# A decoder layer on one core: where q is normalized, when q and k are transposed, and two smaller moves in the order of work

## The chip, the cores and the metric

The kernel runs on one core of a Trainium2 chip. The core has five engines with a queue each: TensorE (PE, matrix products; its weight loads are shown apart as PEld), VectorE (DVE), ScalarE (ACT), GpSimd (POOL) and SyncE (SP, which here issues all DMAs). Each works through its own instructions in order and waits on semaphores for the others. The metric is the device time of one execution in microseconds (us), lower is better.

## The reference, cut to what matters

One layer on x of 256 tokens by 1024 features, float32. Two mixers work side by side, a feed-forward network follows:

```python
h = rmsnorm(x, norm_mix_g)
q, k, v, u_pool, gate_logits = split(h @ w_in)          # 512, 512, 512, 512, 2048 columns
q = rotary(rmsnorm(heads(q), q_norm_g))                 # 8 heads of 64; norm over the 64
k = rotary(rmsnorm(heads(k), k_norm_g))
attn = softmax(causal(q @ k.T * 64**-0.5)) @ v          # 256 tokens are one block, so plain causal attention
pooled = multiscale_pool(u_pool)                        # trailing means over 2, 4, 8, 16 tokens
gates = sigmoid(gate_logits + b_gate)
x = x + (gates[0] * (attn @ w_branch_attn) + gates[1] * (pooled @ w_branch_pool)) @ w_out
h2 = rmsnorm(x, norm_ffn_g)
gate, val = split(causal_conv3(h2 @ w_up))              # 2 x 2816 columns
return x + (silu(gate) * val) @ w_down
```

The norm of q multiplies each head of each token by one number. The rotation is linear and acts within a head, so this number may be applied before it, after it, or to the row of logits.

## The kernel before, in words

**Products.** Activations lie feature by token (128 features on the partitions, 256 tokens along the row), and nearly every weight product is done in three single-pass products: both operands are split into a high part (type fp32r, written by ACT, `high`, line 82) and a low part (the rest, written by DVE, `low`, lines 86 and 88), and `mm3` (lines 94 to 96) adds high by high, high by low and low by high. A product of 128x128 weights by 256 tokens is one PE instruction. Scores, transposes, value products and a few small products are plain float32.

**Weights.** They come in chunks of 1 MB (128x2048). A chunk is split in two pieces of 1024 columns. `next_high` puts a piece's high part on ACT, `next_low` its low part on DVE (one piece behind, STAGGER), and with the last piece of a chunk it issues the DMA of the chunk four places on (`load`). `ahead(n)` does one such pair, and a second one if fewer than n pieces are ready in front of the chunk in use. These calls stand in the program where the author put them, and every engine runs its instructions in exactly this order (the loop at line 714 ties each engine's instructions to program order).

**Stages in order.** q, k and v are projected with tokens on the partitions (`project`). While k and v run, `norm_evacuate` (line 287) takes q and k out of PSUM: ACT squares, DVE multiplies with the token's norm and the gain and sums the squares for each head, POOL raises the mean square to the power -0.5 (line 300), multiplies the 512 columns with it (line 301) and rotates 16 columns of each head (lines 306 to 311). Then come four tiles of pool features (`ps_u`), 16 tiles of gates (`ps_g`, n = 0 to 15), eight tiles of the pool branch (`ps_bp`), eight of the attention branch (`ps_ba`), eight of the output projection (`ps_out`), and the feed-forward stage (`ps_up`, `ps_d`).

**Attention between them.** `to_heads` (line 314) transposes q or k for one half of the tokens: four 128x128 transposes on PE into a bank, one copy on ACT. q's two calls stand after the second `ps_u` tile, k's two after the first gate tile. Before gate tiles 2, 6, 10 and 14 `scores` handles two heads: scores on PE, then on DVE mask, row maximum and the factor -1/8 (lines 438 to 443), on ACT four exponentials with their sums (line 447), on DVE a reciprocal, on POOL the product with it (line 453). Four tiles later `weigh` transposes the result on PE (line 461), and some tiles after that `values` multiplies with v (line 472), and ACT and DVE write `ath` and `atl`. The last `values` comes after the sixth `ps_bp` tile.

**Branches.** Each `ps_ba` tile goes through DVE (line 558, product with the gate), POOL (line 559, sum), ACT (`mh`) and DVE (`ml`), and the output projection reads `mh` and `ml` of all eight tiles: the first two of its tiles run over seven of them before the eighth. `settle` (line 522) is a float32 product ahead of the seventh `ps_bp` tile; its result is read by nobody.

**Residuals.** `residual(j)` (line 577) adds `ps_out` to x on DVE, writes the high part `hhi` and a square on ACT, adds the square to `ss2` on POOL, calls `ahead`, and writes `hlo` on DVE. The first feed-forward tiles run over seven of the eight features, then the token norm R2 is prepared (`ps_n`: line 242, line 245 on POOL, line 249 on DVE, line 253 on PE), then they take the eighth.

PSUM has eight banks of 2 KB a partition: the pool `mm` has four (`bank`), `ps2` two tiles of two banks.

Of the kernel before, what the change touches and what calls it, by code (L numbers as in the profile page):

```python
# [8 lines left out]
F32 = mybir.dt.float32  # L9
F32R = mybir.dt.float32r  # L10
AF = mybir.ActivationFunctionType
ALU = mybir.AluOpType
AX = mybir.AxisListType

P = 128
S = 256
NT = S // P
D = 1024
KD = D // P
H = 8  # L20
DH = 64
AW = H * DH
KA = AW // P
# [7 lines left out]
EPS = 1e-6  # L31
# [20 lines left out]
AHEAD = 4  # L52
FFN_AHEAD = 6
KREADY = 0
FIRST = 2
HOME = 24
LEAD = 104
XCUTS = (1, 2, 3, 4, 6, 8)

# [2 lines left out]
def hybrid_layer_kernel(ctx: ExitStack, tc: tile.TileContext, xq_d, par_d, wkv_d, wpg_d,  # L62
                        wpool_d, wba_d, wbp_d, wout_d, wup_d, wdn_d, out_d):
    nc = tc.nc

    const = ctx.enter_context(tc.tile_pool(name="const", bufs=1))
# [8 lines left out]
    tmp = mixer.enter_context(tc.tile_pool(name="tmp", bufs=2))  # L75

    def bank(name):
        return mm.tile([P, 512], F32, tag="mm", name=name)
# [84 lines left out]
    def ahead(upto=0):  # L163

        next_high()
        next_low()
        if at[1] - sum(p[0] < used[0] for p in pieces) < upto:
            next_high()
            next_low()
# [104 lines left out]
    def project(name, hook, pt=None):  # L274
# [9 lines left out]
            hook(k)  # L284
        return pt

    def norm_evacuate(pt, t, gcol, name):
        r = rtok1[:, t:t + 1]
        g = par[:, None, gcol:gcol + DH].to_broadcast([P, H, DH])
        p3 = pt.rearrange("p (h d) -> p h d", d=DH)  # L290
        qg = tmp.tile([P, 2, 3 * P], F32, tag="big", bufs=4, name=f"qg_{name}{t}")
        qg = qg.rearrange("p a b -> p (a b)")[:, 0:AW].rearrange("p (h d) -> p h d", d=DH)
        q2 = tmp.tile([P, H, DH], F32, tag="q2", bufs=1, name=f"q2_{name}{t}")
        nc.scalar.activation(q2, p3, AF.Square, scale=r)
        nc.vector.scalar_tensor_tensor(qg, p3, r, g, ALU.mult, ALU.mult)
        ss = tmp.tile([P, H], F32, tag="ss", name=f"ss_{name}{t}")
        nc.vector.tensor_reduce(ss, q2, axis=AX.X, op=ALU.add)
        nc.vector.tensor_scalar(ss, ss, 1.0 / DH, EPS, op0=ALU.mult, op1=ALU.add)
        rh = tmp.tile([P, H], F32, tag="rh", name=f"rh_{name}{t}")
        nc.gpsimd.tensor_tensor(rh, ss, mhalf[:, 0:H], ALU.pow)  # L300
        nc.gpsimd.tensor_tensor(qg, qg, rh[:, :, None].to_broadcast([P, H, DH]), ALU.mult)
        cos = par[:, None, C_COS + t * ROPE:C_COS + (t + 1) * ROPE].to_broadcast([P, H, ROPE])
        sin = par[:, None, C_SIN + t * ROPE:C_SIN + (t + 1) * ROPE]
        ta = tmp.tile([P, H, ROPE], F32, tag="ropea", name=f"ra_{name}{t}")
        tb = tmp.tile([P, H, ROPE], F32, tag="ropeb", name=f"rb_{name}{t}")
        nc.gpsimd.tensor_tensor(ta, qg[:, :, 0:ROPE], cos, ALU.mult)
        nc.gpsimd.tensor_tensor(tb[:, :, 0:HALF], qg[:, :, HALF:ROPE],
                                sin[:, :, 0:HALF].to_broadcast([P, H, HALF]), ALU.mult)
        nc.gpsimd.tensor_tensor(tb[:, :, HALF:ROPE], qg[:, :, 0:HALF],
                                sin[:, :, HALF:ROPE].to_broadcast([P, H, HALF]), ALU.mult)  # L310
        nc.gpsimd.tensor_tensor(qg[:, :, 0:ROPE], ta, tb, ALU.add)
        return qg

    def to_heads(qg, t, dst, name):
        pq = bank(f"ps_t{name}{t}")
        flat = qg.rearrange("p h d -> p (h d)")
        for j in range(KA):
            nc.tensor.transpose(pq[:, j * P:(j + 1) * P], flat[:, j * P:(j + 1) * P], ident)
        nc.scalar.activation(dst[:, :, t * P:(t + 1) * P], pq.rearrange("p (j c) -> p j c", c=P), AF.Copy)

    def on_q(k):
        if k % 2 == 1:
# [19 lines left out]
    def on_v(k):  # L342
        if k % 2 == 1:
            ahead()
        if k == 1:
            kg.append(norm_evacuate(ptk[0], 0, C_KG, "k"))
        if k == 3:
            kg.append(norm_evacuate(ptk[1], 1, C_KG, "k"))

    qg, kg, stat = [], [], []  # L350
    ptq = project("q", on_q)
# [56 lines left out]
    for b in range(2):  # L408
        w = chunk("p")
        for c in range(2):  # L410
            ps = feature_tile(w, c, f"u{b}{c}")
            tick()
            ahead()
            pool_group(2 * b + c, ps)
        if b == 0:
            for t in range(NT):
                to_heads(qg[t], t, qT, "q")


    ath = act.tile([P, KA, S], F32R, tag="ath", name="ath")  # L420
# [10 lines left out]
    def scores(hp):  # L431
        ps = ps2.tile([P, 2, 512], F32, tag="ps2", name=f"ps_s{hp}")
        for j in range(2):
            rows = slice(j * DH, (j + 1) * DH)
            nc.tensor.matmul(ps[:, j, P:3 * P], qT[rows, hp, P:S], kT[rows, hp, :], start=True, stop=True)
            nc.tensor.matmul(ps[:, j, 0:P], qT[rows, hp, 0:P], kT[rows, hp, 0:P], start=True, stop=True)
        sm = tmp.tile([P, 2, 3 * P], F32, tag="big", bufs=4, name=f"sm{hp}")
        nc.vector.tensor_tensor(sm, ps[:, :, 0:3 * P],
                                mask.rearrange("p a b -> p (a b)")[:, None, :].to_broadcast([P, 2, 3 * P]), ALU.add)
        mx = tmp.tile([P, 2, 2], F32, tag="mx", name=f"mx{hp}")  # L440
        for t in (1, 0):
            nc.vector.tensor_reduce(mx[:, t, :], sm[:, :, TOK[t]], axis=AX.X, op=ALU.max)
        nc.vector.tensor_scalar(mx, mx, -(DH ** -0.5), None, op0=ALU.mult)
        sums = tmp.tile([P, 2, 2], F32, tag="sums", name=f"sums{hp}")
        for j in range(2):
            for t in (1, 0):
                nc.scalar.activation(sm[:, j, TOK[t]], sm[:, j, TOK[t]], AF.Exp, bias=mx[:, t, j:j + 1],
                                     scale=DH ** -0.5, accum_out=sums[:, t, j:j + 1])
        rs = tmp.tile([P, 2, 2], F32, tag="rs", name=f"rs{hp}")
        nc.vector.reciprocal(rs, sums)  # L450
        for t in (1, 0):
            n = TOK[t].stop - TOK[t].start
            nc.gpsimd.tensor_tensor(sm[:, :, TOK[t]], sm[:, :, TOK[t]],
                                    rs[:, t, :, None].to_broadcast([P, 2, n]), ALU.mult)
        later(4, weigh, hp, sm)
# [46 lines left out]
    for n in range(2 * KD):  # L502
        if n >= FIRST and (n - FIRST) % 4 == 0:
            scores((n - FIRST) // 4)
        if n == 10:
            pool_maps()
            ahead()
        b, c = n // 2, n % 2
        if c == 0:
            w = chunk("g")  # L510
        ps = feature_tile(w, c, f"g{n}")
        if n == KREADY:
            for t in range(NT):
                to_heads(kg[t], t, kT, "k")
        tick()
        ahead(AHEAD if n % 2 else 0)
        nc.vector.tensor_tensor(gate(n), ps[:, 0:S], R1, ALU.mult)
        if n >= 2 * KD - 2:
            sigmoids(3)


    def settle(ps):

        nc.tensor.matmul(ps[:, S:2 * S], ones, diag.rearrange("p t c -> p (t c)"), start=True, stop=True)

    def branch(src, oph, opl, j, w):
        hi, lo = w
        ps = bank(f"ps_b{src}{j}")
        if src == "p" and j == KD - 2:
            settle(ps)  # L530
        for k in range(4):
            sl = slice(k * 512 + (j % 4) * P, k * 512 + (j % 4 + 1) * P)
            mm3(ps[:, 0:S], (hi[:, sl], lo[:, sl]), (oph[:, k, :], opl[:, k, :]), k == 0, k == 3)
        return ps
# [42 lines left out]
    def residual(j, ps):  # L577
        nc.vector.tensor_tensor(xT[:, j, :], ps[:, 0:S], xT[:, j, :], ALU.add)
        g = par[:, C_FFN + j:C_FFN + j + 1]
        high(hhi[:, j, :], xT[:, j, :], g)  # L580
        if j == 0:
            nc.scalar.activation(ss2, xT[:, j, :], AF.Square)
        else:
            s2 = tmp.tile([P, S], F32, tag="s2", name=f"s2_{j}")
            nc.scalar.activation(s2, xT[:, j, :], AF.Square)
            nc.gpsimd.tensor_tensor(ss2, ss2, s2, ALU.add)
        ahead(AHEAD if j % 2 == 0 else 0)
        low(hlo[:, j, :], hhi[:, j, :], xT[:, j, :], g)

    nc.scalar.activation(scrap, ones[:, 0:1], AF.Silu)  # L590
    for b in range(4):
        w = chunk("o")
        ps = [bank(f"ps_out{b}{c}") for c in range(2)]
        if b == 0:

            for ks in (range(KD - 1), range(KD - 1, KD)):
                for c in range(2):
                    tile_part(w, (mh, ml), c, ps[c], ks)
            residual(0, ps[0])
            residual(1, ps[1])  # L600
        else:
            for c in range(2):
                tile_part(w, (mh, ml), c, ps[c], range(KD))
                residual(2 * b + c, ps[c])


    acch, accl = {}, {}
# [177 lines left out]
```

## Time and profile before

| | us |
|---|---|
| three timed runs | 339.91, 340.43, 340.64 (median 340.43) |
| the profiled execution | 340.0 |
| its span, first to last instruction | 338.2 |
| PE busy | 332.9 (98%), 2740 matmul instructions |
| PEld busy | 322.7 (95%) |
| DVE busy | 259.3 (77%) |
| ACT busy | 198.4 (59%) |
| POOL busy | 90.6 (27%) |
| granted TensorE clock | 9 tenths or more in all 40 slices, mean 1.000 |

The 1.8 us between span and time lie around the instructions. A busy PE is not a PE at its fastest: the busy time of a matmul overlaps with the next one, so how fast the stream runs is read from the distance of the starts in the timeline.

### The profile page before, as it was taken

To read this page: it belongs to the slowest core of one execution; us is meant where nothing else is said; L and a number is where in the kernel's file an instruction comes from. 1 tells how busy PE (TensorE), PEld (TensorE's weight loads), DVE (VectorE), ACT (ScalarE), POOL (GpSimd) and SP (SyncE) were. 2 spreads that over 40 slices of the span, in tenths; PEclk is the share of its full clock that TensorE was granted. 3 is DMA by queue.
4 is the path that set the end of the run, shared out by engine and by line. 5 is a ranking of instruction groups with operands and counts; after the bars stand their busy time and mean duration, and the time that the engine had idled before them with its cause. 6 is when DMAs were issued, how large, how long until landed. Compare 5 with 4: busy or idle time off the path is not lost.

```text
span 338.2 us, 6739 instructions
## 1 busy us (share of the span) xinstructions
PE 332.9 (98%) x2740; PEld 322.7 (95%) x2740; DVE 259.3 (77%) x411; ACT 198.4 (59%) x319; POOL 90.6 (27%) x104
## 2 busy tenths in 40 slices
PE   8999999999999999999999999999999999999996
PEld 7888899999999899998999999999999999999995
DVE  4868899796786676798799788777777777777744
ACT  5856624546757954678366565666666565646420
POOL 1006994023204034023222322121212121212130
PEclk9999999999999999999999999999999999999999
DMA  7986462446364372476625565554646363642003
GB/s 264 420 343 240 140 242 118 156 150 236 122 239 134 138 274 82 141 239 242 250 85 200 216 248 161 214 202 174 233 142 248 129 247 128 246 144 107 0 2 124
DMA packets 10399, 62.76 MB, mean 186 GB/s; under 512 B 1153, under 2 KB 2305, under 8 KB 3457
## 3 DMA queue, kind: packets, MB, share of 16 engines
q1 hardware_dynamic: 10368, 62.34, 51.1%
q8 instruction: 21, 0.34, 0.4%
q14 instruction: 10, 0.07, 0.1%
HBM read 61.29 MB, written 1.05 MB: 184 GB/s over the span
## 4 chain that ended last, share of the span: by engine, by line
PE 77%; POOL 8%; DVE 6%; DMA 5%; ACT 2%; issue 1%; SPq 0%; ACTq 0%; POOLq 0%
PE ps_up L95 12%; PE ps_up L94 12%; PE ps_up L96 12%; PE ps_d L646 6%; PE ps_d L647 6%; PE ps_d L648 6%; PE ps_g L94 4%; PE ps_g L96 4%; PE ps_g L95 4%; DMA raw_k<-in_wkv 3%; DVE hlo L88 2%; POOL rh_q L300 2%; DMA xq<-in_xq 1%; POOL rh_k L300 1%; PE ps_ba L95 1%
## 5 line engine op out<-in xcount | busy, mean ns | idle before, releaser
L95 PE MATMUL ps_up<-hlo,hi_up 128*128 128x256 f32 x352 | 97.3, 276 | 0.7 <-DVE hlo L88 0.7
L94 PE MATMUL ps_up<-hhi,hi_up 128*128 128x256 f32 x352 | 97.5, 277 | 0.0
L96 PE MATMUL ps_up<-hhi,lo_up 128*128 128x256 f32 x352 | 97.2, 276 | 0.0
L95 PEld LDWEIGHTS ps_up<-hlo,hi_up 128*128 128x128 f32 x352 | 66.1, 188 | 0.9 <-DVE hlo L88 0.9
L94 PEld LDWEIGHTS ps_up<-hhi,hi_up 128*128 128x128 f32 x352 | 66.1, 188 | 0.0
L96 PEld LDWEIGHTS ps_up<-hhi,lo_up 128*128 128x128 f32 x352 | 66.1, 188 | 0.0
L86 DVE TENSOR_TENSOR lo_up<-raw_up,hi_up 128x1024 fp32r<-128x1024 f32 x44 | 54.8, 1248 | 6.2 <-ACT hi_up L82 6.2
L646 PE MATMUL ps_d<-ah,hi_dn 128*128 128x256 f32 x176 | 48.6, 276 | 0.0
L647 PE MATMUL ps_d<-al,hi_dn 128*128 128x256 f32 x176 | 48.6, 276 | 0.0
L648 PE MATMUL ps_d<-ah,lo_dn 128*128 128x256 f32 x176 | 48.6, 276 | 0.0
L629 POOL TENSOR_TENSOR c_v<-c_g,c_v 128x256 f32<-128x256 f32 x22 | 16.2, 739 | 118.1 <-DVE c_v L612 118.1
L82 ACT ACTIVATE hi_up<-raw_up 128x1024 fp32r<-128x1024 f32 x44 | 45.1, 1046 | 0.0
L82 ACT ACTIVATE ah<-c_v 128x256 fp32r<-128x256 f32 x22 | 9.2, 418 | 45.8 <-POOL c_v L629 45.8
L94 PE MATMUL ps_g<-xhi,hi_g 128*128 128x256 f32 x128 | 35.8, 280 | 0.0
L96 PE MATMUL ps_g<-xhi,lo_g 128*128 128x256 f32 x128 | 35.4, 276 | 0.0
L95 PE MATMUL ps_g<-xlo,hi_g 128*128 128x256 f32 x128 | 35.4, 276 | 0.0
L646 PEld LDWEIGHTS ps_d<-ah,hi_dn 128*128 128x128 f32 x176 | 33.0, 188 | 0.0
L647 PEld LDWEIGHTS ps_d<-al,hi_dn 128*128 128x128 f32 x176 | 33.0, 188 | 0.0
L648 PEld LDWEIGHTS ps_d<-ah,lo_dn 128*128 128x128 f32 x176 | 33.0, 188 | 0.0
L86 DVE TENSOR_TENSOR lo_dn<-raw_dn,hi_dn 128x1024 fp32r<-128x1024 f32 x22 | 27.3, 1241 | 0.4 <-ACT hi_dn L82 0.4
L617 DVE TENSOR_TENSOR u_v<-ps_up,R 128x256 f32<-128x256 f32 x22 | 9.3, 421 | 22.1 <-PE ps_up L96 22.1
L94 PEld LDWEIGHTS ps_g<-xhi,hi_g 128*128 128x128 f32 x128 | 24.0, 188 | 0.4
(185 smaller groups left out, 807.6 us busy)
## 6 DMA issues: line engine op xcount, KB each, us to landing
raw_up<-in_wup SPq DMA_DIRECT2D x22, 1024.0 KB, 4.8
raw_dn<-in_wdn SPq DMA_DIRECT2D x11, 1024.0 KB, 4.8
raw_g<-in_wpg SPq DMA_DIRECT2D x8, 1024.0 KB, 4.8
raw_o<-in_wout SPq DMA_DIRECT2D x4, 1024.0 KB, 4.9
raw_v<-in_wkv SPq DMA_DIRECT2D x2, 1024.0 KB, 13.8
raw_p<-in_wpg SPq DMA_DIRECT2D x2, 1024.0 KB, 6.3
raw_bp<-in_wbp SPq DMA_DIRECT2D x2, 1024.0 KB, 4.7
raw_ba<-in_wba SPq DMA_DIRECT2D x2, 1024.0 KB, 4.8
```

Of the source, the lines that this page charges most:

```text
L82: nc.scalar.activation(hi, src, AF.Copy, scale=scale)
L86: nc.vector.tensor_tensor(lo, src, hi.bitcast(F32), ALU.subtract)
L88: nc.vector.scalar_tensor_tensor(lo, src, scale, hi.bitcast(F32), ALU.mult, ALU.subtract)
L94: nc.tensor.matmul(out, sh, mh, start=start, stop=False, **kw)
L95: nc.tensor.matmul(out, sh, ml, start=False, stop=False, **kw)
L96: nc.tensor.matmul(out, sl, mh, start=False, stop=stop, **kw)
L300: nc.gpsimd.tensor_tensor(rh, ss, mhalf[:, 0:H], ALU.pow)
L617: nc.vector.tensor_tensor(u, ps[:, 0:S], R2, ALU.mult)
L629: nc.gpsimd.tensor_tensor(uc[1], g[1], uc[1], ALU.mult)
L646: nc.tensor.matmul(o, hi[:, sl], acch[i], start=first, stop=False, skip_group_check=True)
L647: nc.tensor.matmul(o, hi[:, sl], accl[i], start=False, stop=False, skip_group_check=True)
L648: nc.tensor.matmul(o, lo[:, sl], acch[i], start=False, stop=i == KF - 1, skip_group_check=True)
```

## The change

Five edits.

1. q is no longer normalized by `norm_evacuate`. Its mean square is kept as sum + 64 EPS in a new constant tile `qs`; after k's second call POOL raises both halves of `qs` to -0.5, which gives 1/8 of the norm's factor, so it holds the logits' 1/8 as well. The row maximum is multiplied by it (a scalar_tensor_tensor in place of a tensor_scalar), and the exponentials take a column of it as their scale in place of the constant 1/8.
2. `to_heads` handles both halves of the tokens in one two-bank tile of `ps2`, and both its calls (q, then k) stand after the first gate tile. The `mm` pool loses these four banks' uses.
3. `settle` is gone.
4. `ahead` is no longer called in the last two `residual`s; `ahead(AHEAD)` and `ahead()` follow the last one.
5. The unused constant `home` shrinks from 24 to 8 columns, as many as `qs` (16) adds.

```diff
-HOME = 24
+HOME = 8
@@
+    qs = const.tile([P, NT, H], F32, name="qs")
@@ norm_evacuate
-        ss = tmp.tile([P, H], F32, tag="ss", name=f"ss_{name}{t}")
-        nc.vector.tensor_reduce(ss, q2, axis=AX.X, op=ALU.add)
-        nc.vector.tensor_scalar(ss, ss, 1.0 / DH, EPS, op0=ALU.mult, op1=ALU.add)
-        rh = tmp.tile([P, H], F32, tag="rh", name=f"rh_{name}{t}")
-        nc.gpsimd.tensor_tensor(rh, ss, mhalf[:, 0:H], ALU.pow)
-        nc.gpsimd.tensor_tensor(qg, qg, rh[:, :, None].to_broadcast([P, H, DH]), ALU.mult)
+        if name == "q":
+            ss = qs[:, t, :]
+            nc.vector.tensor_reduce(ss, q2, axis=AX.X, op=ALU.add)
+            nc.vector.tensor_scalar(ss, ss, 1.0, DH * EPS, op0=ALU.mult, op1=ALU.add)
+        else:
+            ... (as before)
@@ to_heads
-        pq = bank(f"ps_t{name}{t}")
-        flat = qg.rearrange("p h d -> p (h d)")
-        for j in range(KA):
-            nc.tensor.transpose(pq[:, j * P:(j + 1) * P], flat[:, j * P:(j + 1) * P], ident)
-        nc.scalar.activation(dst[:, :, t * P:(t + 1) * P], pq.rearrange("p (j c) -> p j c", c=P), AF.Copy)
+        pq = ps2.tile([P, 2, 512], F32, tag="ps2", name=f"ps_t{name}")
+        for t in range(NT):
+            flat = qg[t].rearrange("p h d -> p (h d)")
+            for j in range(KA):
+                nc.tensor.transpose(pq[:, t, j * P:(j + 1) * P], flat[:, j * P:(j + 1) * P], ident)
+            nc.scalar.activation(dst[:, :, t * P:(t + 1) * P], pq[:, t, :].rearrange("p (j c) -> p j c", c=P), AF.Copy)
@@ on_v, k == 3
+            for t in range(NT):
+                nc.gpsimd.tensor_tensor(qs[:, t, :], qs[:, t, :], mhalf[:, 0:H], ALU.pow)
@@ after the second ps_u tile
-        if b == 0:
-            for t in range(NT):
-                to_heads(qg[t], t, qT, "q")
@@ scores
-        nc.vector.tensor_scalar(mx, mx, -(DH ** -0.5), None, op0=ALU.mult)
+        nc.vector.scalar_tensor_tensor(mx, mx, -1.0, qs[:, :, 2 * hp:2 * hp + 2], ALU.mult, ALU.mult)
@@
-                                     scale=DH ** -0.5, accum_out=sums[:, t, j:j + 1])
+                                     scale=qs[:, t, 2 * hp + j:2 * hp + j + 1], accum_out=sums[:, t, j:j + 1])
@@ after the first gate tile
-            for t in range(NT):
-                to_heads(kg[t], t, kT, "k")
+            to_heads(qg, qT, "q")
+            to_heads(kg, kT, "k")
@@ branch
-        if src == "p" and j == KD - 2:
-            settle(ps)
@@ residual
-        ahead(AHEAD if j % 2 == 0 else 0)
+        if j < KD - 2:
+            ahead(AHEAD if j % 2 == 0 else 0)
@@ after the residuals
+    ahead(AHEAD)
+    ahead()
```

## Rows read from the trace of the kernel before

**Rows 1.** Waits of PE: engine line <- whom, us in total, times, longest.
```profile
PE ps_up L95 <- DVE hlo L88: 0.7, 1, 0.7
PE ps_tk L318 <- POOL qg_k L311: 0.2, 1, 0.2
```

**Rows 2.** Windows, PE: stretch, its us, busy us (instructions), granted clock, DMA.
```profile
163.61:334.70 171.09, 171.09 (x1512) 1.00 0.47 168
```

**Rows 3.** Timeline of PE (start, us, instruction, count), pool branch.
```profile
117.53 0.28 PE L96 MATMUL ps_bp<-poolh,lo_bp 128*128 128x256 f32 x1
...
120.01 0.28 PE L96 MATMUL ps_bp<-poolh,lo_bp 128*128 128x256 f32 x1
```

**Rows 4.** Timeline of PE around the transposes of q and of k.
```profile
44.88 1.04 PE L318 MATMUL ps_tq<-ident,qg_q 128*128 128x128 f32 x8
...
45.88 0.28 PE L95 MATMUL ps_u<-xlo,hi_p 128*128 128x256 f32 x1
...
54.24 0.60 PE L318 MATMUL ps_tk<-ident,qg_k 128*128 128x128 f32 x4
...
55.62 0.28 PE L95 MATMUL ps_g<-xlo,hi_g 128*128 128x256 f32 x1
```

**Rows 5.** Timeline of PE: first tile after scores; settle and the tile after it.
```profile
59.18 0.38 PE L94 MATMUL ps_g<-xhi,hi_g 128*128 128x256 f32 x1
59.40 0.28 PE L95 MATMUL ps_g<-xlo,hi_g 128*128 128x256 f32 x1
...
116.76 0.70 PE L524 MATMUL ps_bp<-diag,ones 128*128 128x256 f32 x2
...
117.42 0.28 PE L95 MATMUL ps_bp<-pooll,hi_bp 128*128 128x256 f32 x1
```

**Rows 6.** Groups of ACT by form: shapes, count, busy us, mean ns, idle before.
```profile
L82 ACT ACTIVATE mh<-xq 128x256 fp32r<-128x256 f32 x8 | 3.3, 416 | 8.5 <-POOL xq L559 8.5
L447 ACT ACTIVATE sm<-sm,mx 128x256 f32<-128x256 f32 x8 | 4.0, 502 | 10.8 <-DVE mx L443 10.8
L620 ACT ACTIVATE c_g<-u_g,par 128x256 f32<-128x256 f32 x22 | 12.9, 586 | 3.2 <-DVE u_g L617 3.2
```

**Rows 7.** Timelines of ACT, DVE and PE, last scores to the output projection.
```profile
103.42 0.51 ACT L447 ACTIVATE sm<-sm,mx 128x256 f32<-128x256 f32 x1 [1.97 <-DVE mx L443]
...
118.71 0.36 ACT L82 ACTIVATE ath<-ps_o 128x256 fp32r<-128x256 f32 x1
...
119.11 0.42 DVE L86 TENSOR_TENSOR atl<-ps_o,ath 128x256 fp32r<-128x256 f32 x1 [1.09 <-ACT ath L82]
...
133.16 0.41 DVE L86 TENSOR_TENSOR ml<-xq,mh 128x256 fp32r<-128x256 f32 x1
...
133.67 0.33 PE L95 MATMUL ps_out<-ml,hi_o 128*128 128x256 f32 x1
```

**Rows 8.** Timelines of DVE, ACT, POOL and PE at the last residuals.
```profile
146.42 0.48 DVE L88 SCALAR_TENSOR_TENSOR hlo<-xq,par,hhi 128x256 fp32r<-128x256 f32 x1
...
154.33 0.51 ACT L82 ACTIVATE hhi<-xq,par 128x256 fp32r<-128x256 f32 x1 [0.58 <-DVE xq L578]
...
155.29 0.73 POOL L586 TENSOR_TENSOR ss<-ss,s 128x256 f32<-128x256 f32 x1 [1.61 <-ACT s L585]
...
155.35 0.95 DVE L88 SCALAR_TENSOR_TENSOR hlo<-xq,par,hhi 128x256 fp32r<-128x256 f32 x1
...
156.36 0.38 PE L95 MATMUL ps_up<-hlo,hi_up 128*128 128x256 f32 x1 [0.70 <-DVE hlo L88]
```

**Rows 9.** Timelines of DVE, POOL and PE: rotation of k; the first softmax.
```profile
51.15 1.27 DVE L401 SCALAR_TENSOR_TENSOR pl<-pw,pu 128x256 f32<-128x256 f32 x1
...
67.32 2.62 POOL L453 TENSOR_TENSOR sm<-sm,rs 128x512 f32<-128x512 f32 x2 [12.38 <-DVE rs L450]
...
70.17 0.82 PE L461 MATMUL ps_p<-ident,sm 128*128 128x128 f32 x6
```

**Rows 10.** Groups of POOL by form: the power for q.
```profile
L300 POOL TENSOR_TENSOR rh_q<-ss_q,mhalf 128x8 f32<-128x8 f32 x2 | 5.3, 2630 | 2.4 <-DVE ss_q L298 2.4
```

More of the change, by code (lines that the diff above doesn't have):

```diff
@@ L295, in norm_evacuate @@
         nc.vector.scalar_tensor_tensor(qg, p3, r, g, ALU.mult, ALU.mult)
-        ss = tmp.tile([P, H], F32, tag="ss", name=f"ss_{name}{t}")
-        nc.vector.tensor_reduce(ss, q2, axis=AX.X, op=ALU.add)
-        nc.vector.tensor_scalar(ss, ss, 1.0 / DH, EPS, op0=ALU.mult, op1=ALU.add)
-        rh = tmp.tile([P, H], F32, tag="rh", name=f"rh_{name}{t}")
-        nc.gpsimd.tensor_tensor(rh, ss, mhalf[:, 0:H], ALU.pow)
-        nc.gpsimd.tensor_tensor(qg, qg, rh[:, :, None].to_broadcast([P, H, DH]), ALU.mult)
+        if name == "q":
[3 more added lines that the diff above has]
+        else:
+            ss = tmp.tile([P, H], F32, tag="ss", name=f"ss_{name}{t}")
+            nc.vector.tensor_reduce(ss, q2, axis=AX.X, op=ALU.add)
+            nc.vector.tensor_scalar(ss, ss, 1.0 / DH, EPS, op0=ALU.mult, op1=ALU.add)
+            rh = tmp.tile([P, H], F32, tag="rh", name=f"rh_{name}{t}")
+            nc.gpsimd.tensor_tensor(rh, ss, mhalf[:, 0:H], ALU.pow)
+            nc.gpsimd.tensor_tensor(qg, qg, rh[:, :, None].to_broadcast([P, H, DH]), ALU.mult)
         cos = par[:, None, C_COS + t * ROPE:C_COS + (t + 1) * ROPE].to_broadcast([P, H, ROPE])
@@ L312, in norm_evacuate, with to_heads @@
         return qg
-    def to_heads(qg, t, dst, name):
-        pq = bank(f"ps_t{name}{t}")
-        flat = qg.rearrange("p h d -> p (h d)")
-        for j in range(KA):
-            nc.tensor.transpose(pq[:, j * P:(j + 1) * P], flat[:, j * P:(j + 1) * P], ident)
-        nc.scalar.activation(dst[:, :, t * P:(t + 1) * P], pq.rearrange("p (j c) -> p j c", c=P), AF.Copy)
+    def to_heads(qg, dst, name):
+        pq = ps2.tile([P, 2, 512], F32, tag="ps2", name=f"ps_t{name}")
[4 more added lines that the diff above has]
+            nc.scalar.activation(dst[:, :, t * P:(t + 1) * P], pq[:, t, :].rearrange("p (j c) -> p j c", c=P), AF.Copy)
     def on_q(k):
@@ L519, in hybrid_layer_kernel @@
             sigmoids(3)
-    def settle(ps):
-        nc.tensor.matmul(ps[:, S:2 * S], ones, diag.rearrange("p t c -> p (t c)"), start=True, stop=True)
     def branch(src, oph, opl, j, w):
```

## The prediction

> **What bounds the kernel now.** I read the engine table first: PE is busy nearly throughout, so only two things can save time, instructions that PE no longer has and moments in which it stands still. The list of waits comes next, PE's rows alone. After the start-up two moderate waits stand there: for `hlo` at the end of the residuals and for k's rotation before its transposes [rows 1]. Third, the timeline of PE, read by the distance of starts. It shows something that the busy time hides: the three-product stream runs at two speeds. In the feed-forward stage it starts an instruction every 0.1133 us (171.09 us over some 1,510; two of the count began before the window) [rows 2]; in the pool and attention branches every 0.118 us (2.48 us for 21) [rows 3]. The granted clock is 1.00 in the fast one, and the page shows full clock in every slice, so it is no matter of the clock. The slow pitch begins where a float32 block is left (after q's transposes, after the last `weigh`, after `settle`) and ends at the next small halt, never by itself. A slow instruction costs 0.0047 us more than a fast one. Fourth, the timelines of DVE, ACT and POOL ahead of each place where PE's next operand is only just in time.
>
> **The change part by part.**
>
> Transposes in one block. q's eight cost 44.88 to 45.88, less the 0.11 at which the stream would have gone on: 0.89 us. k's eight cost 54.24 to 55.62, less 0.11: 1.27 us, with the halt for POOL within [rows 4]. Sixteen in a row cost the first 0.89 and eight more at 0.11 (0.89 / 8, an upper bound): 1.77. Saved: 2.16 - 1.77 = 0.39 us. The pool-feature and gate tiles between the two blocks, 71 instructions at the slow pitch, now follow no float32 block: 71 x 0.0047 = 0.33 us more. If the new block leaves the next tile slow, as q's did, 24 x 0.0047 = 0.11 us is given back. Bounds 0.61 and 0.72; I take 0.65 us. The four copies now come one after the other on ACT behind the block, some 0.5 us each, and scores stand a whole gate tile (2.7 us) later: hidden; without that tile they would cost about 2 us.
>
> POOL. For q it loses two powers (2.63 us each [rows 10]) and two wide products ahead of k, and gets the two powers back behind k. k is ready some 8 us earlier, so its halt goes. `qs` is ready about 52 us into the span (k's end near 55, minus 8, plus 5), and the maximum that wants it is multiplied near 62. Behind that DVE instruction stand weight pieces and gate evacuations, but it does not wait. DVE gains too: the STT of a pool mean takes 1.27 us beside k's product on POOL [rows 9], and POOL's work moves to before much of this.
>
> Exponentials. An ACT instruction on 128x256 takes 416 ns with constants, 502 with one operand per partition (the exponentials' bias), 586 with two (line 620) [rows 6]. The scale becomes the second: 0.085 us each, four for two heads, 0.34 us; bounds 0 (if an exponential hides it) and 0.4. The Trainium skill says the same of the price ("ScalarE: Activation LUTs", section "What ACT_TABLE_LOAD costs": each pointer operand adds about 93 ns); by its figure the four would add 0.37 us, an estimate. No run so far shows an exponential with two.
>
> Where this lands: ACT is gapless from the last heads' exponentials at 103.42 to `ath` at 118.71, which DVE waited for at 119.11; from there a chain of DVE, POOL and ACT runs to the seventh `ml`, written at 133.16 to 133.57, and PE takes it at 133.67, 0.06 us late by the gap after it [rows 7]. PE is not in this chain behind 98 us. So what PE gains between 98 and 133 it waits off at `ml`, and what the chain loses PE loses. The exponentials of the last two heads cost the full 0.34; those of the first six lie beside gate tiles.
>
> `settle`. PE saves 117.42 - 116.76 = 0.66, less 0.22 for a direct entry as after scores: 0.44 us. A direct entry after scores was followed by the fast pitch [rows 5], so 138 instructions may save 0.65 us more. All of this (0 to 1.09 us) lies before `ml`: I count 0. The halt there grows from 0.06 to about 1.4 us.
>
> Weight pieces. Between `hhi` (154.33 to 154.84) and `hlo` (155.35 to 156.30) of the seventh feature DVE does a weight piece. Without it `hlo` starts at about 154.9, and takes 0.48 where POOL is idle and 0.95 where POOL adds [rows 8]. POOL's next sum comes at 155.29, so I take 0.48: ready by 155.4, when PE wants it at 155.49. PE's step to 156.36 and 0.11 of slow re-entry vanish: 0.98 us at most, 0.5 if it takes 0.95. I take 0.95. The Trainium skill has a rule for the two durations ("SBUF — State Buffer", section "SBUF: two separate sides": DVE with two SBUF inputs and GpSimd share a port pair that one holds for a whole instruction). By that rule `hlo` starts before POOL's sum and gets the pair, which is the 0.48 case. What is late next: the two moved pieces, with the one DMA of a weight chunk that SP issues behind them. They come some 2.5 us later, and that chunk is first read over 13 us later; DVE has idle time before the token norm. The token norm's diagonal then has some 0.2 us left before PE.
>
> The maximum's STT for a tensor_scalar and the smaller `home`: nothing, within 0.05 us.
>
> Sum: -0.65 + 0.34 - 0.95 = -1.26 us. Against the profiled execution's 340.0 that is 338.74. This execution lies below the median of the runs, 340.43; the mean of all four is 340.25, and from it I forecast 339.0 us.
>
> **The rivals.**
>
> A, slower: the feed-forward stage inherits the slow pitch. Its 1,510 instructions follow one float32 product (R2's spread at 163 us) without any halt that could end it [rows 2]. Slow throughout it costs 1,510 x 0.0047 = 7.1 us: 339.0 + 7.1 = 346.1. It decides from 0.8 ns an instruction (1.26 / 1,510). For it: of three such products in the trace one (`settle`) left the stream slow, and the change shifts every start before. Against: the other two, the very product in question among them, left it fast, and the instructions from the token norm to it stay the same.
>
> B, no change: one halt takes the place of another. PE reaches the first `weigh` at 70.17, and POOL had its operand at 69.94 [rows 9]. PE now comes 0.65 earlier and the exponentials take 0.34 longer; if DVE gains nothing, PE waits 0.65 + 0.34 - 0.2 = 0.8 us and the first term is gone: -0.65 + 0.8 + 0.34 - 0.95 = -0.5, 339.8. Likewise, `hlo` at 0.95 and a late diagonal leave about 340.0. Against: DVE's crowded stretch (45 to 65 us) is the one that POOL slowed, 2 us by my count of such rows.
>
> C, more: the chain to `ml` isn't rigid, or the exponentials don't grow. Then `settle` and the pitch behind it count: -1.26 - 1.09 - 0.34 = -2.7, 337.6 at the best. For it: the branch tiles also end earlier, and DVE evacuates them. Against: DVE waits for ACT's `ath` there, not for PE [rows 7].
>
> That q's norm in the scale removes no work from PE is certain; its share is only that POOL is done sooner.
>
> **How the numbers follow.** Forecast 0.62, A 0.12, B 0.14, C 0.12. What can be told from no change is 0.2%, 0.7 us. Faster: the forecast nearly whole (its own range 338.4 to 339.6), C, and little of B: 0.75. Same: most of B and a rest: 0.13. Slower: A: 0.12. A range from 337.6 to 340.1 holds the forecast, B and most of C, and leaves A out.
>
> **What would show it.** Right: no row of PE waiting for `qg_k`, the wait for `hlo` gone or under 0.1, sixteen transposes in some 1.8 us, exponentials of 586 ns, and a new wait of PE for `ml`, or for banks in the branch tiles, of over 1 us in all. Wrong: `ml` not waited for (then C), a wait of PE for `sm` (B), a pitch of 0.118 after 163 us (A).

## The result and the profile after

The changed kernel takes 342.01 us (median of five runs, 341.68 to 342.82), the kernel before 340.05 (five runs, 339.91 to 340.64): a ratio of 1.0059, 95% interval 1.0042 to 1.0077. Run again later (experiment 9) it was 340.84 us (12 runs, 340.48 to 342.39) against 340.20, ratio 1.0030 (1.0017 to 1.0042). It is slower by 0.6%, clear of the noise, and the forecast of 339.0 us missed by about 3 us. The profiled execution took 342.01 us, 2.0 more than that of before.

The page of the changed kernel, its engine table:

```profile
PE 334.2 (98%) x2738; PEld 323.8 (95%) x2738; DVE 256.7 (75%) x411; ACT 199.7 (59%) x319; POOL 89.2 (26%) x102
```

Two matmul instructions fewer, and 1.3 us more of PE busy. Its list of PE's waits behind the start-up has two new rows, where [rows 1] had `hlo` and k's rotation:

```profile
PE ps_tk L327 <- ACT qkT L328: 0.8, 1, 0.8
PE ps_tq L327 <- ACT qkT L328: 0.8, 1, 0.8
```

PE's timeline through the new block (start, us, instruction; in brackets the idle time and who ended it), the counterpart of [rows 4]:

```profile
53.01 0.60 PE L327 MATMUL ps_tq<-ident,qg_q 128*128 128x128 f32 x4
54.39 0.63 PE L327 MATMUL ps_tq<-ident,qg_q 128*128 128x128 f32 x4 [0.78 <-ACT qkT L328]
54.85 0.60 PE L327 MATMUL ps_tk<-ident,qg_k 128*128 128x128 f32 x4
56.28 0.63 PE L327 MATMUL ps_tk<-ident,qg_k 128*128 128x128 f32 x4 [0.83 <-ACT qkT L328]
56.67 0.37 PE L94 MATMUL ps_g<-xhi,hi_g 128*128 128x256 f32 x1
56.88 0.28 PE L95 MATMUL ps_g<-xlo,hi_g 128*128 128x256 f32 x1
```

and ACT beside it:

```profile
53.65 0.60 ACT L328 ACTIVATE qkT<-ps_tq 128x512 f32<-128x512 f32 x1 [1.05 <-PE ps_tq L327]
55.05 0.60 ACT L328 ACTIVATE qkT<-ps_tq 128x512 f32<-128x512 f32 x1 [0.81 <-PE ps_tq L327]
55.55 0.59 ACT L328 ACTIVATE qkT<-ps_tk 128x512 f32<-128x512 f32 x1
56.95 0.60 ACT L328 ACTIVATE qkT<-ps_tk 128x512 f32<-128x512 f32 x1 [0.81 <-PE ps_tk L327]
```

Sixteen transposes cost 56.88 - 53.01 - 0.11 = 3.76 us. Four run, ACT copies them (53.65 to 54.25), and only then do the next four begin, at 54.39. So it goes once for q and once for k; between q's second four and k's first, which go to different tiles, there is no wait. Each engine is idle on the other's account in turn: PE waits for ACT's copy, ACT for PE's next four.

From here on PE is 56.88 - 55.62 = 1.26 us behind the kernel before instead of 0.65 ahead. What follows stands beside [rows 6 to 8]. First the group of the exponentials in ACT's table by form (shapes, count, busy us, mean ns, idle before):

```profile
L455 ACT ACTIVATE sm<-sm,mx,qs 128x256 f32<-128x256 f32 x8 | 4.8, 594 | 8.7 <-DVE mx L451 8.7
```

The start of the last heads' exponentials in ACT's timeline:

```profile
105.06 0.60 ACT L455 ACTIVATE sm<-sm,mx,qs 128x256 f32<-128x256 f32 x1 [1.95 <-DVE mx L451]
```

DVE's timeline at the seventh `ml`, and at `hlo` of the sixth and seventh feature:

```profile
135.17 0.41 DVE L86 TENSOR_TENSOR ml<-xq,mh 128x256 fp32r<-128x256 f32 x1
...
154.63 0.96 DVE L88 SCALAR_TENSOR_TENSOR hlo<-xq,par,hhi 128x256 fp32r<-128x256 f32 x1
...
156.51 0.48 DVE L88 SCALAR_TENSOR_TENSOR hlo<-xq,par,hhi 128x256 fp32r<-128x256 f32 x1 [0.58 <-ACT hhi L82]
```

POOL's timeline beside these two `hlo`, and its last sum:

```profile
154.57 0.74 POOL L588 TENSOR_TENSOR ss<-ss,s 128x256 f32<-128x256 f32 x1 [1.61 <-ACT s L587]
156.92 0.74 POOL L588 TENSOR_TENSOR ss<-ss,s 128x256 f32<-128x256 f32 x1 [1.61 <-ACT s L587]
158.32 1.80 POOL L588 TENSOR_TENSOR ss<-ss,s 128x256 f32<-128x256 f32 x1 [0.66 <-ACT s L587]
```

And PE's timeline where it takes the seventh `ml`:

```profile
135.00 0.35 PE L95 MATMUL ps_out<-ml,hi_o 128*128 128x256 f32 x1
...
135.31 0.28 PE L94 MATMUL ps_out<-mh,hi_o 128*128 128x256 f32 x1
135.64 0.39 PE L95 MATMUL ps_out<-ml,hi_o 128*128 128x256 f32 x1
135.86 0.29 PE L96 MATMUL ps_out<-mh,lo_o 128*128 128x256 f32 x1
```

The last heads' exponentials start 105.06 - 103.42 = 1.64 us later than before, the seventh `ml` 135.17 - 133.16 = 2.01 us later, and the execution ends 2.01 us later. PE halts for `ml` behind 135.31 (its next start is 0.33 us later instead of 0.12), and no longer for `hlo`, which takes 0.48 us: POOL's sum comes at 156.92, when it is all but done, while the sixth ran beside the sum at 154.57 and took 0.96. That halt at the end of the residuals cost 0.98 us before, so something behind `ml` must have given it back.

What gave it back is the pitch, the distance from one start of the stream to the next. A view of the same three windows in both kernels shows it (stretch, its us, then for PE, PEld, DVE, ACT and POOL busy us and instructions; granted clock, DMA share, GB/s). The count of PE's instructions in a gapless window is the window over the pitch, plus the two or three that began ahead of it. The changed kernel in gates 10 to 13, in the output projection and in the feed-forward stage:

```profile
87.00:97.00 10.00, 10.00 (x87) 10.00 (x87) 7.19 (x15) 8.05 (x17) 2.41 (x2) 1.00 0.27 95
...
137.00:153.00 16.00, 16.00 (x138) 16.00 (x138) 12.87 (x18) 11.83 (x19) 3.24 (x4) 1.00 0.59 199
166.00:176.00 10.00, 10.00 (x91) 10.00 (x90) 8.29 (x16) 5.22 (x11) 2.64 (x4) 1.00 0.37 148
```

The kernel before in the same windows:

```profile
87.00:97.00 10.00, 10.00 (x91) 10.00 (x90) 7.59 (x14) 7.21 (x16) 2.41 (x2) 1.00 0.30 107
...
137.00:153.00 16.00, 16.00 (x143) 16.00 (x142) 14.59 (x20) 11.77 (x20) 3.03 (x5) 1.00 0.66 213
166.00:176.00 10.00, 10.00 (x91) 10.00 (x90) 8.66 (x16) 5.92 (x12) 3.37 (x4) 1.00 0.24 84
```

87 against 91 and 138 against 143 at a granted clock of 1.00 in all: the changed kernel ran the first two stretches at the slow pitch (0.1178 us by the distance of the starts), the kernel before at the fast one (0.1133 to 0.1135). The feed-forward stage is fast in both.

### The profile page after: what moved, and what is told of

It reads as the page before. It is cut to its first block, busy times and chain, and to the rows that moved or that the text cites. A ratio compares the mean times of both kernels' runs of the same rounds, so it can differ in the third digit from the quotient of the medians.

```text
span 340.2 us, 6730 instructions
## 1 busy us (share of the span) xinstructions
PE 334.2 (98%) x2738; PEld 323.8 (95%) x2738; DVE 256.7 (75%) x411; ACT 199.7 (59%) x319; POOL 89.2 (26%) x102
## 4 chain that ended last, share of the span: by engine, by line
PE 87%; ACT 6%; DVE 3%; POOL 1%; issue 1%; DMA 1%; POOLq 0%; ACTq 0%
PE ps_up L95 12%; PE ps_up L94 12%; PE ps_up L96 12%; PE ps_d L652 6%; PE ps_d L653 6%; PE ps_d L651 6%; PE ps_g L94 4%; PE ps_g L95 4%; PE ps_g L96 4%; PE ps_q L282 3%; PE ps_k L282 3%; PE ps_v L282 3%; PE ps_out L95 2%; PE ps_out L96 2%; PE ps_out L94 2%; ACT xq L490 2%
## 5 line engine op out<-in xcount | busy, mean ns | idle before, releaser
L95 PE MATMUL ps_up<-hlo,hi_up 128*128 128x256 f32 x352 | 97.3, 276 | 0.0
L95 PEld LDWEIGHTS ps_up<-hlo,hi_up 128*128 128x128 f32 x352 | 66.1, 188 | 0.0
L95 PE MATMUL ps_g<-xlo,hi_g 128*128 128x256 f32 x128 | 35.6, 278 | 0.0
```

The lines of the kernel that those rows point to most:

```text
L95: nc.tensor.matmul(out, sh, ml, start=False, stop=False, **kw)
```

## The experiments

"Copies last" stands for the changed kernel with its eight transposes ahead of the two copies.

**1. The copies behind all eight transposes** (on the changed kernel).

```diff
         for t in range(NT):
             ...
                 nc.tensor.transpose(pq[:, t, ...], flat[:, ...], ident)
-            nc.scalar.activation(dst[...], pq[:, t, :]..., AF.Copy)
+        for t in range(NT):
+            nc.scalar.activation(dst[...], pq[:, t, :]..., AF.Copy)
```

> The changed kernel with the order inside the transposing helper turned: all eight transposes of q (or k) first, then the two copies. Theory 1 (the second half's transposes wait because tile and copy are one tile to the dependency tracking, and the copy of the first half stands between them in the program): both waits of PE for the copies go, the block of sixteen takes 1.8 us in place of 3.8, and the time falls by about 2.0 us from 342.0 to 340.0, plus or minus 1 us for the pitch that the stream takes after later float32 blocks. Rival (PE waits for something else that the copies only stand for, such as the bank pair or ACT being late): the wait stays or moves to the next block, and the time stays within 0.7 of 342.0.

Measured: 338.97 us (338.61 to 339.08), before on this chip 340.15; ratio 0.9959 (0.9946 to 0.9973). Its PE timeline at the block:

```profile
52.96 1.04 PE L327 MATMUL ps_tq<-ident,qg_q 128*128 128x128 f32 x8
53.84 1.04 PE L327 MATMUL ps_tk<-ident,qg_k 128*128 128x128 f32 x8
54.63 0.36 PE L94 MATMUL ps_g<-xhi,hi_g 128*128 128x256 f32 x1
54.83 0.28 PE L95 MATMUL ps_g<-xlo,hi_g 128*128 128x256 f32 x1
```

Sixteen transposes in 54.83 - 52.96 - 0.11 = 1.76 us, where the forecast had 1.77, and PE is 55.62 - 54.83 = 0.79 us ahead of the kernel before. Two lines in another order turn the loss into a gain: this version beats both kernels. It is 1 us faster than the theory said, since its output projection ran at the fast pitch and that of the changed kernel at the slow one (144 and 138 instructions in the window above).

**2. A bank for each half, the copy left where it was** (on the changed kernel).

```diff
-        pq = ps2.tile([P, 2, 512], F32, tag="ps2", name=f"ps_t{name}")
         for t in range(NT):
+            pq = bank(f"ps_t{name}{t}")
             ... (transposes and copy use pq[:, ...] in place of pq[:, t, ...])
```

> The changed kernel, where each half's transposes go to a bank of their own (four of the one-bank pool) and the copy still stands right behind its four transposes. Theory 1 (the two halves wait for each other because they are one tile): no wait of PE for the copies, sixteen transposes in 1.8 us, 339.0 like the kernel with the copies last, up to 340.0 if the output projection turns slow. Rival (a copy between two groups of transposes halts PE whatever the tile): both waits of 0.8 us stay and the time is about 342.0.

Measured: 339.10 us (339.01 to 339.79), before 340.56; ratio 0.9962 (0.9949 to 0.9974). Its PE timeline:

```profile
52.96 1.04 PE L327 MATMUL ps_tq<-ident,qg_q 128*128 128x128 f32 x8
53.83 1.13 PE L327 MATMUL ps_tk<-ident,qg_k 128*128 128x128 f32 x8
```

The copies again stand between the two halves, and PE does not wait. So a copy between transposes costs nothing by itself: the wait comes from the shared tile, whose second half is not written until the first half's reader is done, although the two halves are different banks.

**3. The old transposes in the changed kernel** (parts 1, 3 and 4 alone; `to_heads` and its calls as before).

> The changed kernel with the transposes of q and of k in the banks and at the places of the kernel before; q's norm in the exponentials' scale, no settle and the moved weight pieces stay. Theory 1: the whole loss beyond the pitch sits in the block, so this one has the other terms alone: +0.34 (exponentials), -0.39 (k is ready, no halt before its transposes), -0.95 (hlo), 339.0 with the pitch of the kernel before, up to 340.8 if the stream turns slow in the later gate tiles and in the output projection as it did in the changed kernel. Rival (q's norm in the scale makes the gate tiles slow, by its reads or its timing): g10 to g15 are slow here too, at 0.118 us, and the time is 340.5 or more.

Measured: 339.62 us (11 runs, 338.79 to 340.38, in two groups with the gap at 339.1 to 339.5), ratio 0.9982 (0.9970 to 0.9993). Without part 2 the change is a small gain; the loss lies in part 2. (Its profile, of a run in the upper group, has gates 10 to 13 at the slow pitch, 87 instructions, and the output projection at the fast one, 143.)

**4. The weight pieces alone** (before, with part 4).

```diff
-        ahead(AHEAD if j % 2 == 0 else 0)
+        if j < KD - 2:
+            ahead(AHEAD if j % 2 == 0 else 0)
...
+    ahead(AHEAD)
+    ahead()
```

> The kernel before with the moved weight pieces alone. My forecast's term: the wait for hlo (0.98 us with its re-entry) goes, 340.05 - 0.95 = 339.1. Rival (the pieces come back as a wait for the diagonal of the token norm, or hlo takes 0.95 beside POOL): 339.6 to 340.1. If the stream enters the token norm's products in another phase, the feed-forward stage could turn slow: 346.

Measured: 339.89 us (11 runs, 339.37 to 341.16), ratio 0.9992 (0.9983 to 1.0001): nothing that can be told. DVE's timeline at `hlo` of the seventh feature:

```profile
154.68 0.48 DVE L88 SCALAR_TENSOR_TENSOR hlo<-xq,par,hhi 128x256 fp32r<-128x256 f32 x1 [0.58 <-ACT hhi L82]
```

Its window of the output projection:

```profile
137.00:153.00 16.00, 16.00 (x138) 16.00 (x138) 14.60 (x20) 11.96 (x20) 3.22 (x5) 1.00 0.67 221
```

The wait is gone as forecast, and the slow pitch (138) took it back in this execution, as in the changed kernel. Yet this stretch begins some 20 us ahead of the first instruction that part 4 moves.

**5. `settle` alone taken out** (before).

> The kernel before without the settle product alone. My forecast's term: PE arrives earlier and waits it off at ml, so nothing: 340.05 plus or minus 0.2, with a halt of about 1 us of PE before the seventh ml. Rival 1 (the gain counts): 340.05 - 1.05 = 339.0. Rival 2 (settle set the pitch of what follows: without it, or with the longer halt, the output projection runs at 0.118 us): the 190 instructions up to the last residual cost 0.9 us more, of which the wait for hlo hides up to 0.9, so 340.0 to 340.9.

Measured: 340.07 us (11 runs, 339.82 to 340.52), ratio 0.9995 (0.9987 to 1.0004). PE's timeline at the seventh `ml`:

```profile
133.17 0.28 PE L94 MATMUL ps_out<-mh,hi_o 128*128 128x256 f32 x1
133.49 0.38 PE L95 MATMUL ps_out<-ml,hi_o 128*128 128x256 f32 x1
133.72 0.28 PE L96 MATMUL ps_out<-mh,lo_o 128*128 128x256 f32 x1
```

The product cost 0.44 us of PE, and PE waits it off: its step at `ml` is 0.32 us in place of 0.12, and three branch tiles ahead are entered with steps of 0.21, 0.21 and 0.17. Worth nothing, as forecast, though the halt at `ml` is not the 1 us expected.

**6. A scale operand alone** (before, with the exponentials' 1/8 read from a constant tile).

```diff
+    eighth = const.tile([P, 16], F32, name="eighth")
+    nc.gpsimd.memset(eighth, DH ** -0.5)
...
-                                     scale=DH ** -0.5, accum_out=...)
+                                     scale=eighth[:, t * H + 2 * hp + j:...], accum_out=...)
```

> The kernel before; the exponentials' scale is read from a constant tile of 1/8 with one column for each head and half, nothing else. My forecast's term: 256-column exponentials of 586 to 600 ns in place of 502, the chain to the seventh ml and PE with it 0.35 us later, 340.15 + 0.35 = 340.5. Rival 1 (an exponential hides it): 340.15. Rival 2 (the longer exponentials are what turns the gate tiles 10 to 15 slow): these run at 0.118 us and 0.47 us more is lost before the last scores, 341.0.

Measured: 341.00 us (11 runs, 340.87 to 341.19), before 340.56; ratio 1.0013 (1.0004 to 1.0022), so +0.44 us. Its exponentials, in the groups of ACT:

```profile
L449 ACT ACTIVATE sm<-sm,mx,eighth 128x256 f32<-128x256 f32 x8 | 4.8, 595 | 10.9 <-DVE mx L445 10.9
```

595 ns against the 502 of [rows 6]: 0.093 each, 0.37 for the last four, the price that the forecast took. The chain behind them shows it too: from the last heads' first exponential to the seventh `ml` it is 134.07 - 103.96 = 30.11 us here, 133.16 - 103.42 = 29.74 before. The +0.44 of the time is not this term alone, for the profile has gates 10 to 13 slow as well (87 instructions, some 0.4 us), as the second rival said. That the longer exponentials cause this is not borne out: experiment 7 has the same ones and these tiles fast.

**7. q's norm in the scale alone** (before, with part 1).

> The kernel before with q's norm in the exponentials' scale alone; transposes, settle and weight pieces as before. Forecast's terms: -0.39 (k is ready) + 0.35 (exponentials) = about 340.1 if the gate tiles 10 to 15 stay fast. If q's norm in the scale is what turns them slow, as in all three kernels with it so far: PE and the chain behind it lose 106 x 0.0044 = 0.47 us more, 340.6.

Measured: 339.93 us (8 runs, 339.51 to 340.13), before 340.56; ratio 0.9980 (0.9969 to 0.9990). Its window of gates 10 to 13 is fast:

```profile
87.00:97.00 10.00, 10.00 (x91) 10.00 (x90) 7.18 (x14) 7.59 (x16) 2.41 (x2) 1.00 0.29 107
```

So this edit does not by itself make those tiles slow. It has the same dear exponentials as experiment 6 and is 1.07 us faster. Two things account for most of it: the first stretch was slow in experiment 6 (87 instructions in the same window, some 0.4 us), and PE's wait for `hlo` is 0.2 us here and 0.7 there.

**8. Float32 products put into the stream** (on "copies last": a 128x128x256 product that nobody reads ahead of gate tile 11 and one in the output projection, to see whether it switches the pitch).

> The changed kernel with the copies last, and two more float32 products of 128x128 by 256 whose results nobody reads: ahead of gate tile 11, and in the output projection behind the first two tiles' seven features. Theory: such a product inside the running stream leaves it fast, as the token norm's does in every profile so far: gate tiles 11 to 13 run at 0.1133 (0.36 us less) for a price of 0.44, and the output projection is fast behind the second, price 0.44: 338.97 + 0.08 + 0.44 = 339.5. Rival (the pitch behind such a product is chance): g11 to g13 stay at 0.118 and the time is 339.9 or more.

Measured: 339.97 us (9 runs, 339.49 to 341.34), ratio 0.9984 (0.9973 to 0.9995). Inconclusive: both stretches were fast already ahead of the products (starts 0.114 us apart) and stayed fast behind them.

**9, 10, 11. The changed kernel again, "copies last" with part 4 undone, and "copies last" again**, side by side on one chip.

> The changed kernel as it is, beside the next two on one chip, and a second profile of it. Theory: the two waits for the copies (0.8 us each) and the slow pitch in the output projection (214 instructions, 117.8 ns apart) belong to this order of instructions: 342.0 +- 0.4, both seen again, 3.0 us behind the kernel with the copies behind the transposes. Rival: the slow pitch of the output projection was the chance of one execution; then this profile shows it at 113.2 ns and some runs lie near 341.0.

> The kernel with the copies behind the transposes, but with the weight pieces between the last two residuals again (part 4 undone). Theory: PE waits 0.7 us for hlo again, and hlo takes 0.95 us beside POOL's sum; at the same pitch in the output projection it is 0.95 us slower than with part 4: 339.0 + 0.95 = 339.95. Rival: part 4 is worth nothing because what it gains is waited off behind it (token norm): 339.0. Second rival: the pitch in the output projection changes with it; then the profile shows 117.8 ns in one of the two, and the difference is 0 or 2.

> The kernel with the copies behind the transposes once more, as the partner of the two others on this chip: 339.0 +- 0.3, with its output projection at 113.2 ns if the pitch goes with the order of instructions.

Measured, with before at 340.20 us: the changed kernel 340.84 (7 of its 12 runs from 340.48 to 340.96, five from 341.51 to 342.39); part 4 undone 339.47 (11 runs, 339.14 to 339.93), ratio 0.9978 (0.9969 to 0.9986); copies last 339.36 (10 runs, 338.65 to 340.29), ratio 0.9975 (0.9965 to 0.9984). The changed kernel's waits for the copies are there again, and it is 1.5 us behind "copies last" by the medians, 1.9 by the means (341.18 and 339.33).

"Copies last" in experiment 1, by the windows used above:

```profile
87.00:97.00 10.00, 10.00 (x87) 10.00 (x86) 7.22 (x14) 7.58 (x16) 2.42 (x2) 1.00 0.28 107
...
137.00:153.00 16.00, 16.00 (x144) 16.00 (x143) 14.81 (x20) 12.16 (x20) 3.69 (x5) 1.00 0.66 227
```

The same kernel in experiment 11:

```profile
87.00:97.00 10.00, 10.00 (x91) 10.00 (x90) 7.22 (x14) 7.59 (x16) 2.42 (x2) 1.00 0.30 107
...
123.00:132.00 9.00, 9.00 (x82) 9.00 (x81) 6.59 (x13) 4.08 (x8) 5.72 (x7) 1.00 0.50 194
...
137.00:153.00 16.00, 16.00 (x138) 16.00 (x137) 14.81 (x20) 12.29 (x20) 3.84 (x5) 1.00 0.63 228
```

One program, and both stretches have changed sides: slow then fast in one execution, fast then slow in the other. The changed kernel did the same in its first stretch: 90 instructions in the second profile, 87 in the first (its output projection was slow in both, 138). So the pitch of these stretches does not go with the order of instructions. It is settled anew, at least from one session and chip to another; that it also differs between runs of one session is suggested by the two groups of runs, and only argued. The expectation that "copies last" keeps a fast output projection fell. The fence above shows one thing more: in experiment 11 PE still ran fast up to 132 us (82 instructions in 9 us), halted for `ml` between 132.37 and 133.69, and ran slow from there on. Here the slow pitch began at a small halt.

In experiment 10 PE's timeline at the residuals shows what part 4 is worth there:

```profile
155.41 0.28 PE L94 MATMUL ps_up<-hhi,hi_up 128*128 128x256 f32 x1
155.92 0.39 PE L95 MATMUL ps_up<-hlo,hi_up 128*128 128x256 f32 x1 [0.23 <-DVE hlo L88]
156.14 0.28 PE L96 MATMUL ps_up<-hhi,lo_up 128*128 128x256 f32 x1
```

PE loses (155.92 - 155.41) + (156.14 - 155.92) - 0.23 = 0.50 us, half of what [rows 8] showed, since DVE is earlier against PE: `hlo` is ready 155.86 - 155.41 = 0.45 us after PE's last start ahead of it, 156.30 - 155.38 = 0.92 before. Between the medians of experiments 10 and 11 stand 0.11 us, against the 0.95 expected: the pitch of the output projection (some 0.94 us) is worth twice the edit.

## Why the prediction was wrong, step by step

The sum against the two profiled executions, 342.01 and 340.0 us:

| term | forecast | measured | from |
|---|---|---|---|
| transposes, and the pitch between them | -0.65 | +1.26 | `ps_g` product of L95 behind the block, 56.88 and 55.62 |
| pitch of gates 10 to 13 | 0 | +0.38 | last exponentials +1.64, less 1.26 |
| exponentials | +0.34 | +0.37 | `ml` +2.01, less 1.64 |
| `settle` | 0 | 0 | experiment 5 |
| wait for `hlo` | -0.95 | -0.98 | halt gone |
| pitch of the output projection | 0 | +0.98 | what is left; 214 x 0.0044 = 0.94 |
| sum | -1.26 | +2.01 | |

The last term is what the others leave, so the sum agrees by construction; the count of 214 instructions is what supports it.

**The step that failed** is the first, where it says: "The four copies now come one after the other on ACT behind the block, some 0.5 us each, and scores stand a whole gate tile (2.7 us) later: hidden". They do not stand behind the block (and take 0.60 us each). Line 328 is inside the loop over the halves, so in program order q's first copy stands ahead of q's second four transposes; and those write the tile that this copy reads. I asked who waits for the copies (scores, hidden) and not what the copies make wait. The diff had it in plain sight: a loop that writes, reads and writes one tile where there had been a tile for each half. The price, 3.76 - 1.77 = 1.99 us, is two rounds of PE to ACT and back. It is the whole error of this term: the gate tile behind the block ran fast, which is the forecast's bound of -0.72, and -0.72 + 1.99 = +1.27. With the copies moved or the tiles parted the block costs 1.76 us: the arithmetic of the block held, the order did not.

**The second error is about the pitch.** Read from one execution, "begins where a float32 block is left" and "ends at the next small halt" were taken for rules of this program. In the changed kernel the slow pitch of the output projection outlasts the halts at 135.00 and 135.31, and the same kernel comes out fast or slow in the same stretch. In experiment 11 the slow pitch even began at such a halt. So nothing for gates 10 to 13 and nothing for the output projection were certainties about stretches that vary by 0.4 and 0.9 us. The 0.33 us counted for the tiles between the two old blocks did come: these tiles ran slow (0.1177 to 0.1179) in all six profiles that have q's transposes ahead of them and fast (0.1134 to 0.1136) in all seven that have not, and PE reached the new block at 53.01, where 54.24 - 0.89 - 0.33 = 53.02 had been counted. Over the thirteen profiles gates 10 to 13 are slow in five (87 instructions in their window) and the output projection in four (138). Those four all have part 4, as have four of the nine fast ones; since the stretch begins before part 4 can act, I read that as chance, which so few profiles do not prove. What decides the pitch of the stretches that vary stays open.

**What held.** k's rotation is ready and its wait gone; the exponentials grew by 92 ns, a little over the 85 taken. The second operand's price is the one that the Trainium skill states ("ScalarE: Activation LUTs", section "What ACT_TABLE_LOAD costs", about 93 ns for each pointer operand), and experiment 6 agrees with it at 93. The chain from the last heads' first exponential to the seventh `ml` does not hang on PE, as the forecast said: it took 29.74 or 29.75 us in the three profiles with a constant scale and 30.08 to 30.12 in the ten others, whichever pitch PE ran at, and `settle` was worth nothing. The halt of about 1.4 us at `ml` did not come: PE's step there is 0.33 us. Part of the gain went elsewhere: the 95 instructions from 102.3 to 113.4 us ran slow here, at 95 x 0.0044 = 0.42 us. `hlo` took 0.48 us; the one that began 0.06 us behind POOL's sum took 0.96. This agrees with the Trainium skill's rule on the shared port pair ("SBUF — State Buffer", section "SBUF: two separate sides"). The forecast left out what the moved pieces do to POOL's last sum: beside them it took 1.80 us instead of 0.74 (it starts at 158.32). In the changed kernel it still ended 0.95 us ahead of PE's product that reads it (161.07), in experiment 1 only 0.08 us (158.11 and 158.19): part 4 has hardly more to give.

**The rivals.** A fell: the feed-forward stage ran 90 or 91 instructions in its 10 us window in all thirteen profiles. B did not happen: no row of PE waits for `sm`, and `hlo` came at 0.48. The changed kernel could not put its first half to the test, since PE came 1.26 us later and not 0.65 earlier; experiment 1 does, with PE 0.79 us ahead at the block, and there too no row waits for `sm`. C fell with experiments 5 and 6: without `settle` nothing was gained, and the exponentials grew. None was about the new block itself, the one place where the change made PE and ACT alternate; a rival there ("the halves wait for each other's copies: two copies and their way there and back, about 2 us", the price that the prediction itself gave to unhidden copies) would have ended at 341.0.

## What to carry to other kernels

When tiles are merged, go through the merged tile's writers and readers in program order: a reader between two writers is a round trip between engines, here 1 us each, even where they touch different banks; put all writes first, or keep a tile for each half. A term that rests on a pitch read from one execution is a range, not a value: profile the same kernel in two sessions before a microsecond is booked to it. And an edit that moves a copy is asked both questions, who waits for it and whom it makes wait.

## What the runs showed of the hardware

At a granted clock of 1.00 the three-product stream starts an instruction about every 0.1134 us or about every 0.1178. It holds the slow one for up to 214 instructions and the fast one through the whole feed-forward stage, some 1,510. In gates 10 to 13 and in the output projection the same program took either. The slow one was not ended by the halts for `ml` in the changed kernel (starts 0.19 and 0.33 us apart), and began at such halts in experiment 11. Behind q's eight transposes it was slow in six profiles out of six. Behind the float32 product in the token norm, at the start of the feed-forward stage, it was fast thirteen times out of thirteen.
